# Mixing gates by seven block products inside attention, branch outputs and gates in DRAM, PSUM in single banks

## The chip, the cores and the metric

The kernel runs on one core of one Trainium2 chip. The metric is the device time of one execution in microseconds (us). The core's engines run side by side, each with an instruction queue of its own: PE (TensorE, matrix products; PEld is its weight load), DVE (VectorE), ACT (ScalarE), POOL (GpSimd) and SP (SyncE, which issues DMAs here). SBUF is the memory on the core that the engines read and write. PSUM holds what PE writes, in eight banks of 512 float32 columns on each of 128 partitions. DRAM is reached by DMA alone.

## The reference, cut to what matters

One layer works on 128 prompt tokens and 512 latent tokens of width D = 1024, all in float32:

```
h = x * (1 + scale) + shift                       # from a conditioning vector
z = h @ w_in                                      # 1024 -> 10240
hy, g_h, qkv, g_a, m = split(z)                   # 3072, 1024, 3072, 1024, 2048
y_h = hyena_long_conv(short_conv(hy))             # gated long convolution by a Fourier transform
y_a = context_attention / neighbourhood_attention # 16 heads of 64; latent queries also attend to cached keys
p_h = (y_h * silu(g_h)) @ w_bh
p_a = (y_a * silu(g_a)) @ w_ba
m_h, m_a = split(sigmoid(m))
out = (m_h * p_h + m_a * p_a) @ w_out
x_new = layer_norm(ALPHA * x + gate * out)
```

The change is about `m`: two thousand and forty-eight columns of the product `h @ w_in`, the mixing gates of the two branches.

## The kernel before, in words

**Numbers and tiles.** The 640 tokens lie in the free dimension, and features on the 128 partitions. Each float32 operand is held as two halves in a shorter format that PE takes at full rate (F32R): a high half, and the low half that is left of it. A product is three passes, high by high, high by low and low by high. The modulated input is `hH` and `hL`, each 128 x 8 x 640, where the 8 are its blocks of 128 features.

The weights are 104 tiles (`wall`) of 128 outputs by 1024 inputs. Tile numbers: 0 to 31 for the convolution inputs and `g_h`, 32 (`T_Q`) and up for queries, keys, values, `T_GA` for the attention gate, 64 to 71 (`T_MH`) and 72 to 79 (`T_MA`) for the two mixing gates, 80 to 87 (`T_BH`) for `w_bh`, 88 to 95 (`T_BA`) for `w_ba`, 96 to 103 (`T_WO`) for `w_out`. `wraw` loads a tile, 512 KB, by SP into one of two buffers; `wtile` splits it (`split`): ACT copies the high half `wh` (L98), DVE subtracts for the low half `wl` (L99). The loads wait for a free buffer, which the splitting of an older tile gives.

`proj` makes one output tile of 128 x 640 from one weight tile: for each of 8 blocks k, three passes by two halves of 320 tokens, 48 matmuls of 128 x 320 at L166, into one PSUM tile of two banks (`ps_mm`, two such tiles). It yields after each k, so that another generator's work can be put between. The other four banks (`ps_ax`) are "aux" banks, for scores, transposes and the like. `weave(main, side, n, m)` runs two generators in proportion, and so writes the program with pieces of `side` between those of `main`.

**The stages.** After a start that computes the modulation come four quarters of the convolution branch, whose results `yh0` to `yh7` stay in SBUF. Then comes attention, two heads for each j = 0 to 7 ("head j" below stands for such a pair), from 391 to 669 us. For each j, `attend(j)` is woven with plain projections, `mains(j)`: queries, keys, values and gates of coming heads, and for j = 7 the eight tiles 64 to 71 (`mix_h`), whose results stay in SBUF as `mh0` to `mh7`. In attention PE follows the written order (a `manual_schedule` for PE); the queues of DVE, ACT, POOL and SP are ordered by a scheduler from its own model, so that there an instruction can stand elsewhere than where it is written.

`attend` takes two blocks of 128 queries at a time. `tiled` writes the scores of two blocks and two heads into the four aux banks; for each, `probs` adds the bias and takes the row minimum on DVE (L803), exponentiates on ACT (L806), inverts the sum on DVE (L807) and multiplies on POOL (L808). The next step, `turned`, transposes these probabilities on PE into the same four banks, and ACT copies them out (L826). PE does 36 matmuls of `mains` between one such step and the next. `gated` (L868) multiplies a head's output by its gate into `ya0` to `ya7`, in SBUF too.

**After attention** (669 us on): two tiles of `mix_a` (72, 73) while ACT and DVE split `yh`; then eight `w_bh` tiles over `yh`, each gated by `mh`, with `ya` split beside them and the modulation's gate rows (L236) between; then eight `w_ba` tiles over `ya` with the remaining `mix_a` tiles between; then the output projection (L1065) from weights that take over the place of `hH` and `hL`, and the norm. The gate of such a tile is one ACT and one DVE instruction over both banks:

```python
ps = (yield from proj(T_MH + n))[2]                     # [2]: both banks as one tile
nc.scalar.activation(two(th), ps[:, :, :HALF], AF.Tanh, scale=0.5)
...
nc.vector.scalar_tensor_tensor(two(th), two(th), 1.0, ps[:, :, :HALF], op0=ALU.add, op1=ALU.mult)
```

Of the kernel before, what the change touches and what calls it, by code (L numbers as in the profile page):

```python
# [18 lines left out]
NK = 8  # L19
# [26 lines left out]
def tile_hyena_natten_step(ctx: ExitStack, tc: tile.TileContext, a, o):  # L46
# [44 lines left out]
    ps_mm = ctx.enter_context(tc.tile_pool(name="ps_mm", bufs=2, space=PSUM))  # L91
    ps_ax = ctx.enter_context(tc.tile_pool(name="ps_ax", bufs=4, space=PSUM))

    def aux(name):
        return ps_ax.tile([P, 512], F32, tag="aux", name=name)

# [8 lines left out]
    out = {"yh": {}}  # L105

# [48 lines left out]
    def bank(i, ps_pair=None):  # L155
        if ps_pair:
            return (*ps_pair, None)
        both = ps_mm.tile([P, 2, 512], F32, tag="mm", name=f"mm{i}")
        return both[:, 0], both[:, 1], both
# [301 lines left out]
    def conv_tile(i, dst):  # L461
        lo, hi, _ = yield from proj(i, eng="dma")
# [12 lines left out]

    def gate_tile(i, dst, eng=None):
        ps = (yield from proj(i, eng=eng))[2]
        nc.scalar.activation(two(dst), ps[:, :, :HALF], AF.Tanh, scale=0.5)
        nc.vector.scalar_tensor_tensor(two(dst), two(dst), 1.0, ps[:, :, :HALF], op0=ALU.add, op1=ALU.mult)
# [17 lines left out]
    def gate_conv(n):  # L497
        if n in half_done:
            gapped_product(out["yh"][n], out[f"u{n // 2}"][n % 2])
        half_done.add(n)  # L500
# [150 lines left out]
    yh, ident = out["yh"], out["ident"]  # L651
# [20 lines left out]
    def queries(j):  # L672
        lo, hi, _ = yield from proj(T_Q + j)
# [10 lines left out]
    def keys(j):  # L684
        raw = const.tile([P, 196], F32, tag="pack1", name=f"ck{j}")[:, :P]
        load_to(raw, a["ck"][j])
        lo, hi, _ = yield from proj(T_K + j)
# [18 lines left out]
    def values(m):  # L706
        w = [wtile(T_V + 2 * m + i, width=256) for i in range(2)]
        ps = ps_mm.tile([P, 2, 512], F32, tag="mm", name=f"v{m}")
# [7 lines left out]
        for half in range(2):  # L716
            ks = range(4 * half, 4 * half + 4)
            for k in ks:
                for x, wk, first, last in passes(k):
                    for t in range(4):  # L720
                        nc.tensor.matmul(  # L721
                            ps[:, t // 2, t % 2 * 256 : t % 2 * 256 + 256], x[:, k, P * t : P * t + P], wk,
                            start=first and t % 2 == 0, stop=last, skip_group_check=True,
                        )
                yield
            if half:
                nc.scalar.activation(v[:, :1024], ps[:].rearrange("p a b -> p (a b)"), AF.Copy)
            else:
                pe = ps_mm.tile([P, 2, 512], F32, tag="mm", name=f"ve{m}")[:, 0]
# [21 lines left out]
    ya, tms, edges, biases = [], [], {}, {}  # L751

    def attention_setup():
        nonlocal at, mask
        hy.close()
        yap = out["yap"] = tail.enter_context(tc.tile_pool(name="yap", bufs=1, side="right"))
        ya.extend(row(yap, "ya", f"ya{j}", bufs=NK) for j in range(NK))
# [15 lines left out]
    at = mask = None  # L773
# [22 lines left out]
    def probs(j, b, s, tm):  # L796
        lo, hi = TWIN[b]
        res = []
        for h in range(2):
# [3 lines left out]
            nc.vector.tensor_tensor_reduce(  # L803
                pv, s[h][:, : hi - lo], tm[h][:, lo:hi], 1.0, 3.0e38, ALU.add, ALU.min, accum_out=sm[:, 0:1]
            )
            nc.scalar.activation(pv, pv, AF.Exp, scale=-1.0, bias=sm[:, 0:1], accum_out=sm[:, 1:2])  # L806
# [60 lines left out]
    def gated(j, cols, o_):  # L867
        nc.vector.tensor_tensor(ya[j][:, cols], out[f"sg{j}"][:, cols], o_, op=ALU.mult)  # L868

    def block_values(n, o_):  # L870
# [5 lines left out]
        if b < 3:  # L876
            gated(j, slice(192 + P * b, 320 + P * b), o_)
        else:
            gated(j, slice(576, NT), o_[:, :64])
            gated(j, B7, o_[:, 64:])  # L880

    def prompt_values(j, o_):
        for h in range(2):
            pvm(o_[rows(h)], val(j, 0, h), head[j]["ptp"][:, h * P : h * P + P], True, True)
        gated(j, slice(PC, PC + LP), o_)
# [46 lines left out]
    def mix_h():  # L932
        homes = ((0, "q"), (0, "k"), (0, "v"), (), (0, "ql"), (0, "kl"), (1, "q"), (1, "ql"))
        for n in range(NK):
            th = slot(*homes[n], f"mh{n}") if homes[n] else th
            th, pair = (pair[:, NT:], None) if n == 3 else (th[:, :NT], th)
            ps = (yield from proj(T_MH + n))[2]
            nc.scalar.activation(two(th), ps[:, :, :HALF], AF.Tanh, scale=0.5)
            out[f"mh{n}"] = th
            yield  # L940

    weave(hand_over(), chain(long_conv(3), long_conv_back(3), attention_setup()), 6 * NK + N_VALUES, N_CONV + N_BACK + 1)

    def mains(j):
        if j < 3:
            return (gate_a(j + 1), queries(j + 2), keys(j + 2)), 3 * NK
        return {
            3: ((values(2), queries(5)), NK + N_VALUES),
            4: ((gate_a(4), keys(5), queries(6)), 3 * NK),
            5: ((gate_a(5), keys(6), values(3)), 2 * NK + N_VALUES),  # L950
            6: ((gate_a(6), queries(7), keys(7), gate_a(7)), 4 * NK),
            7: ((mix_h(),), 7 * NK),
# [8 lines left out]

    mp = tail.enter_context(tc.tile_pool(name="mp", bufs=1, side="right"))
    lp = left.enter_context(tc.tile_pool(name="lp", bufs=1))
    gpart = slot(1, "v", "gpart")[:, :D]
    yhH = [row(lp, "yhH", f"yhH{n}", F32R, NK) for n in range(NK)]
    yhL = []
    yaH = [row(mp, "yaH", f"yaH{n}", F32R, NK) for n in range(NK)]
    yaL = []

    def gate_rows():  # L970
        for pair in range(2):
            ps = aux(f"gate{pair}")
            for i in range(4):
                raw = wp.tile([P, D], F32, tag="raw", name=f"gate{pair}{i}")
                ada(16 + 4 * pair + i, ps[:, i * P : i * P + P], raw[:])
# [3 lines left out]
    def mix_a(n):  # L979
        ps = now(proj(T_MA + n))[2]  # L980
        th = mp.tile([P, NT], F32, tag="th", bufs=3, name=f"mta{n}")
        nc.scalar.activation(two(th[:]), ps[:, :, :HALF], AF.Tanh, scale=0.5)
# [3 lines left out]
    mtas = [mix_a(0), mix_a(1)]  # L986
    for n in range(NK):
        yhL.append(row(yhp, "yh", f"yhL{n}", F32R))
        split(yhH[n][:], yhL[n][:], yh[n][:])
    for n in range(NK):  # L990
        th = out[f"mh{n}"]
# [249 lines left out]
```

## Time and profile before

| | |
|---|---|
| median of 3 runs | 925.89 us (925.84 to 927.05) |
| the profiled execution | 925.7 us, of which the profile's span is 923.9 us |
| granted TensorE clock, mean over the span | 0.997 |
| idle time of DVE, ACT, POOL in the span | 47%, 59%, 84% |
| DMA, mean over the span | 102.13 MB, 111 GB/s |
| stages, us from the start of the span | attention 391 to 669; `mix_a` 0 and 1 to 700; `w_bh` tiles to 756; `w_ba` and the other `mix_a` to 872; output projection and norm to 924 |

The page is taken from one execution. A row of a stretch of time gives its length, and then for each engine its busy time and, in brackets, its instructions. A group row names the line, the engine, the operation and its tiles, out<-in without the numbers at their ends; "x8" is a count. In the chain each row is a start in us, a length in us, and what ran.

### The profile page before, as it was taken

The numbers are of one execution on the slowest core, as the hardware profiler recorded it, in microseconds if no ns is written. First come the engines' busy times: TensorE is split into PE (matmuls) and PEld (weight loads), VectorE is DVE, ScalarE is ACT, GpSimd is POOL, SyncE is SP. The second block draws the span as 40 slices with busy tenths as digits, with TensorE's granted clock in tenths as the row PEclk, the third lists the DMA queues.
The fourth block names the chain that finished last, engine by engine and source line by source line (L and its number), as shares of the span: only waits on it lengthen the run. The fifth ranks groups of instructions, "written<-read, shape, count | busy, mean of one in ns | idle before, by whom it ended". The sixth has DMA issues, their size and how long they took to land.

```text
span 923.9 us, 16758 instructions
## 1 busy us (share of the span) xinstructions
PE 910.2 (99%) x6856; PEld 877.4 (95%) x6856; DVE 486.4 (53%) x948; ACT 380.4 (41%) x776; POOL 146.2 (16%) x188
## 2 busy tenths in 40 slices
PE   8999999999999999999999999999999999999996
PEld 7899999999999999999999999999999999999885
DVE  4776775693796676445352533432261223335676
ACT  4485455554545334255454544444261112223200
POOL 0011010110010000474454543331000000000000
PEclk9999999999999999999999999999999999999998
DMA  8966664655465113242222221212123343224631
GB/s 320 380 161 135 128 149 98 137 133 123 100 141 126 50 49 85 86 122 67 71 68 69 67 70 58 72 49 70 48 69 113 120 146 99 72 69 116 205 114 69
DMA packets 36553, 102.13 MB, mean 111 GB/s; under 512 B 4316, under 2 KB 13020, under 8 KB 36477
## 3 DMA queue, kind: packets, MB, share of 16 engines
q1 hardware_dynamic: 32300, 86.35, 28.9%
q0 software_dynamic: 4032, 14.68, 9.8%
q8 instruction: 54, 0.88, 0.4%
q14 instruction: 23, 0.18, 0.1%
q10 hardware_dynamic: 144, 0.03, 0.0%
HBM read 97.38 MB, written 3.67 MB: 109 GB/s over the span
## 4 chain that ended last, share of the span: by engine, by line
PE 95%; DVE 2%; ACT 2%; issue 1%; POOL 0%; POOLq 0%
PE mm L166 65%; PE out L1065 6%; PE v L721 5%; PE s L788 2%; PE s L831 2%; PE pt L824 2%; PE ve L732 1%; PE adaT L236 1%; PE adaT L253 1%; PE yb L151 1%; PE yb L153 1%; PE yb L152 1%; PE gate L236 0%; PE fl L384 0%; PE fl L385 0%
## 5 line engine op out<-in xcount | busy, mean ns | idle before, releaser
L166 PE MATMUL mm<-hH,wh 128*128 128x320 f32 x1120 | 263.3, 313 | 0.9 <-ACT hH L312 0.6
L166 PE MATMUL mm<-hH,wl 128*128 128x320 f32 x1120 | 259.7, 310 | 0.4 <-DVE wl L99 0.4
L166 PE MATMUL mm<-hL,wh 128*128 128x320 f32 x1120 | 259.1, 310 | 0.0
L99 DVE TENSOR_TENSOR wl<-raw,wh 128x1024 fp32r<-128x1024 f32 x66 | 81.6, 1237 | 231.9 <-ACT wh L98 231.7
L166 PEld LDWEIGHTS mm<-hH,wh 128*128 128x128 f32 x1120 | 186.7, 188 | 6.2 <-issue 4.2
L166 PEld LDWEIGHTS mm<-hH,wl 128*128 128x128 f32 x1120 | 188.0, 188 | 1.4 <-DVE wl L99 1.1
L166 PEld LDWEIGHTS mm<-hL,wh 128*128 128x128 f32 x1120 | 188.2, 188 | 1.1 <-DVE hL L313 0.5
L98 ACT ACTIVATE wh<-raw 128x1024 fp32r<-128x1024 f32 x66 | 69.8, 1059 | 216.8 <-PE mm L166 95.9
L143 POOL DMA_DIRECT2D wl<-wall x28 | 24.3, 869 | 264.0 <-ACT wl L142 208.8
L144 ACT ACTIVATE wh<-raw 128x1024 fp32r<-128x1024 f32 x28 | 29.7, 1060 | 42.9 <-PE mm L166 42.7
L808 POOL TENSOR_SCALAR p<-p,sm 128x384 f32<-128x384 f32 x32 | 42.1, 1326 | 27.7 <-DVE sm L807 27.7
L1095 POOL TENSOR_TENSOR r<-r,bc 128x64 f32<-128x64 f32 x1 | 0.3, 320 | 249.7 <-ACT r L1094 249.7
L808 POOL TENSOR_SCALAR edge<-edge,sm 128x320 f32<-128x320 f32 x32 | 35.5, 1121 | 0.0
L474 DVE SCALAR_TENSOR_TENSOR x<-zs,pack,x 128x641 f32<-128x641 f32 x32 | 28.3, 884 | 12.1 <-ACT x L472 12.0
L826 ACT ACTIVATE pts<-pt 128x384 f32<-128x384 f32 x64 | 26.2, 502 | 11.0 <-PE pt L824 11.0
L142 ACT ACTIVATE wl<-raw 128x1024 fp32r<-128x1024 f32 x28 | 30.0, 1071 | 0.0
L166 PE MATMUL mm<-yhH,wh 128*128 128x320 f32 x128 | 29.9, 315 | 0.0
L166 PE MATMUL mm<-yaH,wh 128*128 128x320 f32 x128 | 29.2, 309 | 0.0
L166 PE MATMUL mm<-yhL,wh 128*128 128x320 f32 x128 | 29.2, 309 | 0.0
L166 PE MATMUL mm<-yaH,wl 128*128 128x320 f32 x128 | 29.2, 309 | 0.0
L166 PE MATMUL mm<-yaL,wh 128*128 128x320 f32 x128 | 29.2, 309 | 0.0
L166 PE MATMUL mm<-yhH,wl 128*128 128x320 f32 x128 | 29.2, 309 | 0.0
(330 smaller groups left out, 1677.7 us busy)
## 6 DMA issues: line engine op xcount, KB each, us to landing
raw<-wall SPq DMA_DIRECT2D x96, 512.0 KB, 3.6
wl<-wall POOLq DMA_DIRECT2D x28, 512.0 KB, 5.8
ada<-wada SPq DMA_DIRECT2D x16, 512.0 KB, 8.1
gate<-wada SPq DMA_DIRECT2D x8, 512.0 KB, 3.7
wo<-wall SPq DMA_DIRECT2D x8, 512.0 KB, 3.7
xt<-xT SPq DMA_DIRECT2D x8, 320.0 KB, 8.1
dec<-decay SPq DMA_DIRECT2D x20, 128.0 KB, 3.5
x<-xB SPq DMA_DIRECT2D x5, 512.0 KB, 3.8
```

Source lines behind the costliest of these rows:

```text
L98: hi = nc.scalar.activation(dst_h, src, AF.Copy)
L99: return hi, (eng or nc.vector).tensor_tensor(dst_l, src, f(dst_h), op=ALU.subtract)
L142: nc.scalar.activation(wl, raw[:], AF.Copy, scale=-1.0)
L143: nc.gpsimd.dma_start(wl, a["wall"][i], accum_op=ALU.add)
L144: nc.scalar.activation(wh, raw[:], AF.Copy)
L166: nc.tensor.matmul(ps[hf][:, :HALF], wt[k], x[:, hf * HALF : (hf + 1) * HALF], start=(i == 0 and k == 0), stop=(i == lead[2] and k == NK - ...
L474: nc.vector.scalar_tensor_tensor(d, zs[:, c : c + NG], convw[:, i, c : c + 1], d, op0=ALU.mult, op1=ALU.add)
L721: nc.tensor.matmul(ps[:, t // 2, t % 2 * 256 : t % 2 * 256 + 256], x[:, k, P * t : P * t + P], wk, start=first and t % 2 == 0, stop=last, ...
L788: nc.tensor.matmul(dst[h], x[rows(h), qs], y[rows(h), ks], start=i == 0, stop=i == 2, skip_group_check=True)
L808: nc.gpsimd.tensor_scalar_mul(pv, pv, sm[:, 2:3])
L826: nc.scalar.activation(ptS[:], pt[:, :384], AF.Copy)
L1065: ins = nc.tensor.matmul(dst, m[k][:, c0 : c0 + P], w[:, c : c + n], start=(first and k == 0), stop=(last and k == NK - 1), skip_group_che ...
```

## The change

Three things are altered.

*Sixteen mixing-gate tiles become eight pairs.* Two weight tiles (256 outputs) by 1024 inputs are seen as a 2 x 2 grid of blocks: a11 and a12 are the first tile's inputs 0 to 511 and 512 to 1023, a21 and a22 the second tile's. The tokens are seen so too: b11, b12 are inputs 0 to 511 of tokens 0 to 319 and of 320 to 639, b21, b22 the same tokens with inputs 512 to 1023. Strassen's scheme in Winograd's form gives the 2 x 2 result by seven block products instead of eight, from four sums of weight blocks, four sums of token blocks (`t1` to `t4`) and additions of the products. The token sums don't depend on the tile; they are made once, one half (`r` = 0 and 1) beside head 0 and head 1, and kept as high and low halves. A pair (`pair_tile`) then loads two weight tiles, makes four weight sums of 128 x 512 (L1007) and splits seven blocks (L101 on ACT, L102 on DVE), does seven products of 4 k by 3 passes into four banks x, y, v, z (the last three products are added to x, v, z), copies x out on ACT (L1041) and makes five additions on DVE (L1043, L1049) ahead of four tanh (L1061). The eight pairs stand inside attention: one beside each of heads 2 to 6, three beside head 7, where the eight tiles 64 to 71 were; nothing of tiles 72 to 79 is left after attention.

*Branch outputs and gates are kept in DRAM.* `yh` is stored after its quarter, `ya` by blocks in `gated` (L884, L885), the gates by ACT's queue (L1062); each is loaded again where it is used after attention.

*Each PSUM tile is a single bank* (`acc`, four of them in the place of two double ones), so a projection has two tiles, and what was one instruction over both banks is now two (L481 and L486 for gates).

Line numbers of the changed kernel are some 2 to 210 higher: L168 for the plain matmul, L813, L818, L819, L820 for the steps of `probs`, L1247 for the output projection. The core of the diff:

```diff
-    ps_mm = ctx.enter_context(tc.tile_pool(name="ps_mm", bufs=2, space=PSUM))
+    ps_mm = ctx.enter_context(tc.tile_pool(name="ps_mm", bufs=4, space=PSUM))
...
-    def gated(j, cols, o_):
-        nc.vector.tensor_tensor(ya[j][:, cols], out[f"sg{j}"][:, cols], o_, op=ALU.mult)
+    def gated(j, o_, *spans):
+        yo = tp.tile([P, P], F32, tag="yo", bufs=3, name=f"yo{j}")
...
+            nc.vector.tensor_tensor(yo[:, c0 : c0 + n], out[f"sg{j}"][:, cols], o_[:, c0 : c0 + n], op=ALU.mult)
+            (nc.scalar if j == 7 else nc.sync).dma_start(ya_d[j][:, cols], yo[:, c0 : c0 + n])
...
+    def token_sums(r):
...
+        tc.keep_in_program_order(nc.vector.tensor_tensor(t1, part(hH, 0, 1), part(hL, 0, 1), op=ALU.add))
+        yield
+        nc.vector.tensor_tensor(t2, t1, part(hH, 0, 0), op=ALU.subtract)
+        nc.vector.tensor_tensor(t2, t2, part(hL, 0, 0), op=ALU.subtract)
+        yield
+        keep("t1", t2)
...
+    ORDER = ("b11", "t2", "t3", "t1", "b21", "t4", "b22")
...
+        def prep(j):
+            if j > 6:
+                return
+            wb[j] = wp.tile([P, 2, 512], F32R, tag=RING[j % 5], bufs=2 if RING[j % 5] == "wh" else 3, name=f"wb{i0}_{j}")
+            split(wb[j][:, 0], wb[j][:, 1], src[j])
...
+        for j in range(7):
+            if j < 4:
+                ps["xyvz"[j]] = acc(f"sp{i0}_{j}")[:, :HALF]
+            dst, x = ps["xyvzxvz"[j]], operand(ORDER[j])
+            for k in range(4):
+                wh, wl = (wb[j][:, i, P * k : P * k + P] for i in range(2))
+                for i, (wk, xi) in enumerate(((wh, 0), (wh, 1), (wl, 0))):
+                    nc.tensor.matmul(
+                        dst, wk, x(xi, k), start=j < 4 and k == 0 and i == 0, stop=k == 3 and i == 2, skip_group_check=True,
+                    )
+                if k == 1:
+                    yield
+            if j == 0:
+                u = halfrow("u", 1, "u")
+                nc.scalar.activation(u, dst, AF.Copy)
+            elif j == 1:
+                nc.vector.tensor_tensor(u, dst, u, op=ALU.add)
+            elif j == 4:
+                use(0, 0, dst)
+            else:
+                if j != 3:
+                    c = halfrow("c", 4, f"c{j}_")
+                nc.vector.tensor_tensor(c, dst, c if j == 3 else u, op=ALU.add)
+                if j != 2:
+                    use(*{3: (1, 1), 5: (1, 0), 6: (0, 1)}[j], c)
+            prep(j + 5)
...
-            7: ((mix_h(),), 7 * NK),
+            3: ((mix(1), values(2), queries(5)), NK + N_VALUES + N_PAIR),
...
+            7: ((mix(5), mix(6), last_pair(mix(7))), 3 * N_PAIR),
...
-    mtas = [mix_a(0), mix_a(1)]
...
+        th = mixed(mh_d, n, "mh", NK)
...
-            for k in range(NK):
+            for k in (0, 1, 2, 3, 4, 6, 7, 5):
```

Three places show how instructions stand in the queues. A name is that of a tile with the numbers of the tile itself and of its allocation at its end. The first is DVE's queue beside head 0, from the second pair of score blocks on; `s2`, `s3` are scores, `p` and `edge` probabilities, `sm` row statistics. Before:

```order
L803 ISA p0_0_2_4569,sm0_0_2_4570<-s2_0_4553,tm0_4014 128x384
L803 ISA sm0_0_2_4570 128x1
L803 ISA p0_1_2_4575,sm0_1_2_4576<-s2_1_4554,tm1_4018 128x384
L803 ISA sm0_1_2_4576 128x1
L803 ISA edge30_4044,sm0_0_3_4581<-s3_0_4555,tm0_4014 128x320
L803 ISA sm0_0_3_4581 128x1
L803 ISA edge31_4046,sm0_1_3_4586<-s3_1_4556,tm1_4018 128x320
L803 ISA sm0_1_3_4586 128x1
L807 RECIPROCAL sm0_0_2_4570<-sm0_0_2_4570 128x1
L703 TENSOR_TENSOR kl2_4749<-ck2_4691,k2_4748 128x128 x2
```

In the changed kernel the same stretch of DVE's queue reads so, with `ts00` and `ts01` the token sums in the making and `t1_01`, `t3_01` low halves of finished ones:

```order
L102 TENSOR_TENSOR t1_01_4713<-ts01_4684,t1_00_4712 128x640
L813 ISA p0_0_2_4637,sm0_0_2_4638<-s2_0_4621,tm0_4073 128x384
L813 ISA sm0_0_2_4638 128x1
L813 ISA p0_1_2_4643,sm0_1_2_4644<-s2_1_4622,tm1_4077 128x384
L813 ISA sm0_1_2_4644 128x1
L956 TENSOR_TENSOR ts01_4684<-ts01_4684,hH_82 128x640
L102 TENSOR_TENSOR t3_01_4790<-ts00_4683,t3_00_4789 128x640
L712 TENSOR_TENSOR kl2_4844<-ck2_4773,k2_4843 128x128 x2
L819 RECIPROCAL sm0_0_2_4638<-sm0_0_2_4638 128x1
L956 TENSOR_TENSOR ts01_4684<-ts01_4684,hL_83 128x640
L819 RECIPROCAL sm0_1_2_4644<-sm0_1_2_4644 128x1
L813 ISA edge30_4103,sm0_0_3_4649<-s3_0_4623,tm0_4073 128x320
```

Sums of 640 columns now stand before the four reductions and between them; the key differences `kl2`, which stood behind the last of the four, stand between the second and the third.

The second place is DVE's queue beside head 7, behind the last reciprocals; `ov16` holds attention outputs. Before:

```order
L807 RECIPROCAL sm7_0_3_7475<-sm7_0_3_7475 128x1
L807 RECIPROCAL sm7_1_3_7480<-sm7_1_3_7480 128x1
L99 TENSOR_TENSOR wl68_7617<-raw68_7614,wh68_7616 128x1024
L99 TENSOR_TENSOR wl69_7690<-raw69_7687,wh69_7689 128x1024
L868 TENSOR_TENSOR ya7_4008<-sg7_7121,ov16_0_7627 128x128
L868 TENSOR_TENSOR ya7_4008<-sg7_7121,ov16_1_7628 128x128
L99 TENSOR_TENSOR wl70_7771<-raw70_7768,wh70_7770 128x1024
L99 TENSOR_TENSOR wl71_7849<-raw71_7846,wh71_7848 128x1024
```

In the changed kernel DVE's queue there holds the second and third of the last three pairs, with `u76`, `c2_76` the additions of the pair of tiles 76 and 77, and `s2_78`, `s1_78` the weight sums of the pair of 78 and 79:

```order
L1043 TENSOR_TENSOR u76_8465<-sp76_1_8470,u76_8465 128x320
L102 TENSOR_TENSOR wb76_5_8467<-raw77_8428,wb76_5_8467 128x512
L102 TENSOR_TENSOR wb76_6_8484<-s1_76_8432,wb76_6_8484 128x512
L1049 TENSOR_TENSOR c2_76_8529<-sp76_2_8487,u76_8465 128x320
L1007 TENSOR_TENSOR s2_78_8618<-raw78_8614,raw79_8616 128x512
L1007 TENSOR_TENSOR s1_78_8620<-s2_78_8618,raw79_8616 128x512
L1049 TENSOR_TENSOR c2_76_8529<-sp76_3_8531,c2_76_8529 128x320
L102 TENSOR_TENSOR wb78_0_8622<-raw78_8614,wb78_0_8622 128x512
```

The weight sums of the third pair stand between two additions of the second pair, and read `raw78` and `raw79`, which a load brings; the gating of `ya7` stands later in the queue.

The third place is PE's queue where the branch projections begin, after attention. Before, from the last matmuls of tile 73 to the first of tile 80:

```order
L166 MATMUL mm73_7990<-hL_77,wh73_7986 128x320 x2
L166 MATMUL mm73_7990<-hH_76,wl73_7987 128x320 x2
L166 MATMUL mm80_8071<-yhH0_7911,wh80_8067 128x320 x2
L166 MATMUL mm80_8071<-yhL0_8041,wh80_8067 128x320 x2
L166 MATMUL mm80_8071<-yhH0_7911,wl80_8068 128x320 x2
L166 MATMUL mm80_8071<-yhH1_7912,wh80_8067 128x320 x2
L166 MATMUL mm80_8071<-yhL1_8044,wh80_8067 128x320 x2
L166 MATMUL mm80_8071<-yhH1_7912,wl80_8068 128x320 x2
L166 MATMUL mm80_8071<-yhH2_7913,wh80_8067 128x320 x2
```

In the changed kernel PE's queue, near the end of the first two branch tiles, reads so:

```order
L168 MATMUL mm80_0_8870<-yhs14_8853,wl80_8867 128x320
L168 MATMUL mm80_1_8871<-yhs14_8853,wl80_8867 128x320
L168 MATMUL mm81_0_8945<-yhs15_8854,wh81_8941 128x320
L168 MATMUL mm81_1_8946<-yhs15_8854,wh81_8941 128x320
L168 MATMUL mm81_0_8945<-yhs14_8853,wl81_8942 128x320
L168 MATMUL mm81_1_8946<-yhs14_8853,wl81_8942 128x320
L238 MATMUL gate0_8930<-gate00_8931,st_84 32x128 x8
L168 MATMUL mm82_0_9019<-yhs0_8649,wh82_9015 128x320
L168 MATMUL mm82_1_9020<-yhs0_8649,wh82_9015 128x320
```

After attention the scheduler orders PE too. It has interleaved tiles 80 and 81, which now end together; the eight matmuls of the first gate row follow, and then tile 82; the `mix_a` tiles that stood ahead of them are gone.

More of the change, by code (lines that the diff above doesn't have):

```diff
@@ L930, in gate_a @@
         yield
[L932 to L939, printed above, removed]
[L940 to L942 removed]
+    SUMS = ("t1", "t3", "t2", "t4")
```

273 lines of the change are left out of this document (196 added, 77 removed).

## The prediction

> **What bounds the kernel now.** I read the head of the page, then the busy time of each engine, then the chain that ended last.
>
> ```profile
> span 923.9 us, 16758 instructions
> PE 910.2 (99%) x6856; PEld 877.4 (95%) x6856; DVE 486.4 (53%) x948; ACT 380.4 (41%) x776; POOL 146.2 (16%) x188
> PE 95%; DVE 2%; ACT 2%; issue 1%; POOL 0%; POOLq 0%
> PE mm L166 65%; PE out L1065 6%; PE v L721 5%; PE s L788 2%; PE s L831 2%; PE pt L824 2%; PE ve L732 1%; PE adaT L236 1%; PE adaT L253 1%; PE yb L151 1%; PE yb L153 1%; PE yb L152 1%; PE gate L236 0%; PE fl L384 0%; PE fl L385 0%
> ```
>
> TensorE is busy or on the chain nearly throughout, and two thirds of the span are the plain projections of L166. A busy PE could still be a slow PE, so I looked at what a matmul costs in the chain in order of time, and at the stages by stretches (columns: length; busy us of PE, PEld, DVE, ACT, POOL; granted clock; DMA share; GB/s).
>
> ```profile
> 405.90 10.57 PE mm L166 x72
> 485.22 1.44 PE ve L732 x12
> 487.97 5.76 PE v L721 x48
> ```
>
> ```profile
> 390.70:669.20 278.50, 277.89 (x2306) 267.74 (x2305) 105.35 (x359) 127.96 (x340) 112.07 (x121) 1.00 0.23 69
> 700.10:756.40 56.30, 56.30 (x462) 53.56 (x461) 13.31 (x14) 7.67 (x9) 0.00 (x0) 1.00 0.39 131
> 872.00:923.90 51.90, 43.60 (x212) 36.24 (x210) 35.39 (x69) 3.20 (x7) 0.93 (x2) 0.94 0.28 101
> ```
>
> A 320-column matmul costs 10.57 / 72 = 0.1468 us in a row, at clock 1.00. In attention (first row) PE idles 0.6 us of 278.5, with DVE at 38%, ACT at 46%, POOL at 40%. After attention (second row) nothing else comes near. Only the last 52 us hold 8.3 us of PE idle, and the change does not touch that code's dependencies. So the rate is PE's, and what counts is matmuls removed and waits put in their place.
>
> **What it removes.** The 16 mixing-gate tiles took 16 x 48 = 768 matmuls; eight pairs of 7 products x 4 k x 3 passes take 672, of the same 128x320 shape, each with its own weight load as before (6856 and 6856 above). 96 x 0.1468 = **14.1 us** off PE. A product sends twelve matmuls in a row into one bank, where a plain tile alternates between two. The twelve ve matmuls also share one bank, at 1.44 / 12 = 0.120 us each; the v matmuls alternate, at 5.76 / 48 = 0.120. Both ends that these rows give are nothing, so I price it at nothing; that one bank costs more all the same is a rival below.
>
> The Trainium skill, "TensorE: Matmul & The Clock Gate", section Back-to-back issue gap, gives a warm isolated gap of N/2.4 + 2.5 ns, 136 ns for 320 columns. The trace has 147, and decides. By the page the saving would be 13.0 us, and the sum below 1.1 us higher.
>
> **What it adds on DVE and ACT.** Durations: mean ns of one, by shape; the L1024 and lower rows give min/median/max.
>
> ```profile
> L1024 DVE TENSOR_TENSOR mta<-mta,mh x8: 819/821/825, 775.4 to 862.8; 128x640 f32<-128x640 f32 x8
> L99 DVE TENSOR_TENSOR wl<-raw,wh x66: 1218/1226/1651, 11.8 to 846.5; 128x1024 fp32r<-128x1024 f32 x66
> L99 DVE TENSOR_TENSOR sl<-sd,sh x20: 678/687/694, 61.2 to 318.8; 128x512 fp32r<-128x512 f32 x20
> L681 DVE SCALAR_TENSOR_TENSOR ql<-mm,q 128x320 fp32r<-128x320 f32 x6 | 2.9, 481 | 0.0
> L98 ACT ACTIVATE sh<-sd 128x512 fp32r<-128x512 f32 x20 | 12.8, 638 | 17.6 <-DVE sd L390 11.7 <-PE yb L152 5.9
> L470 ACT ACTIVATE zs<-mm 128x320 f32<-128x320 f32 x23 | 10.5, 458 | 0.0
> ```
>
> Token sums: 13 operations of 640 columns per half, 2 x 13 x 0.82 = 21.3 us of DVE. A pair: 4 weight sums and 7 low halves at 0.687, 5 result additions at 0.481: 9.96 us, against 2 x 1.23 for two plain tiles. ACT per pair: 7 x 0.638 + 5 x 0.458 = 6.8 us. Attention then runs about 277.9 - 6 x 7.05 (the mixing tiles inside the first row) + 8 x 84 x 0.1468 = 334 us of PE, with 105 + 21 + 80 - 10 + 3 = 199 us of DVE: 60%. On average that is cover enough; the places where it is not are local. Gate evacuations in two halves add 0.2 us of ACT to each of 16 tiles, under a full PE. Three edits cost nothing for the same reason: yh, ya and both gates through DRAM (about 21 MB over 500 us, 42 GB/s on 69 to 131 now; without that cover each would be one late load, the 3.7 us below), single banks (as many banks as before), and the final weights' order.
>
> **The places where PE can wait.**
>
> *Heads 0 and 1 (token sums).* After a pair of score blocks PE runs 36 matmuls, then needs all four score banks back for its transposes.
>
> ```profile
> 390.67:400.33 9.66, 9.66 (x77) 9.02 (x77) 6.31 (x26) 4.96 (x18) 6.18 (x10) 1.00 0.56 163
> 404.37 0.22 PE ptp L912 x2
> 416.47:431.50 15.03, 15.03 (x128) 14.41 (x128) 7.28 (x25) 7.47 (x24) 6.93 (x8) 1.00 0.20 61
> 431.50:436.03 4.53, 4.53 (x52) 4.17 (x53) 3.02 (x16) 2.11 (x6) 1.67 (x3) 1.00 0.24 82
> 439.81 0.22 PE ptp L912 x2
> ```
>
> Head 0: DVE ended the reductions at 400.33, 4.0 us ahead of the transposes. Nine token operations now stand before the last reduction and the ck remainder too: 9 x 0.82 + 0.5 = 7.9 us, of which 9.66 - 6.31 = 3.35 fall into DVE's idle time. 7.9 - 3.35 - 4.0 = 0.5 us of wait. Head 1: eleven token operations and two weight differences are added to 7.28 us: 7.28 + 9.0 + 1.4 = 17.7 in 15.03, 2.7 over, against 3.8 us of room (436.03 to 439.81). No wait by that count; I take 0.5 since two instructions of those fourteen can wait for loads. Each: 0 to 3.0 (3.0 if the idle time can't be used). The exponentials, queued behind the reductions on ACT, and POOL's multiplications behind them have a whole further round of slack.
>
> *Pairs beside heads 2 to 6.* A pair's last two products add into banks that DVE must have read first. By the queue's order the reductions of four score blocks (about 4.5 us) stand before that reading, which leaves some 3 us. 0.5 us in all, 0 to 2.0.
>
> *The three pairs in a row at the end.* Between 613 and 669 the attention pieces of the chain sum to 13.1 us; with 252 matmuls PE has 50 us there, DVE 29.9 for the pairs + 7.7 for the head + 4.1 for yh and the next weights = 41.7: 83%. The third pair's weight differences stand in DVE's queue ahead of a result addition of the second, and wait for a load that is issued only when the second's weights are split:
>
> ```profile
> raw<-wall SPq DMA_DIRECT2D x33, 512.0 KB, 3.7
> ```
>
> On SP those loads now stand behind six stores of yo that wait for DVE. Count for the second pair: the addition is ready about when product 7 needs its bank. I take 1.0 us, 0 (all hidden) to 4.0 (one whole load).
>
> *First branch tile.* PE starts two branch tiles interleaved, so both weight buffers come free together; the third waits for a split (1.06 + 1.23 us) under six matmuls, eight gate matmuls and four more, about 2.0 us. 0.4 us, 0 to 1.5.
>
> Sum, against the profiled execution's own 925.7 us (span 923.9): 925.7 - 14.1 + 0.5 + 0.5 + 0.5 + 1.0 + 0.4 = 914.5; the median shown is 0.2 above that execution, so **914.7**. All low ends: 911.8; all high ends: 925.3.
>
> **The rivals.**
>
> *DVE and POOL hold each other up.* Rows that speak for it:
>
> ```profile
> L808 POOL TENSOR_SCALAR edge<-edge,sm x32: 1074/1083/2013, 399.8 to 640.1; 128x320 f32<-128x320 f32 x32
> L808 POOL TENSOR_SCALAR p<-p,sm x32: 1232/1244/2252, 401.9 to 637.9; 128x384 f32<-128x384 f32 x32
> ```
>
> Most are at the median, a few run up to 1.0 us longer, and the wl row above has a maximum 0.43 us over its median. The new sums and splits all read two SBUF tiles. If each met a POOL operation with 40% (POOL's share) and waited half of it, 0.22 us: at the crowded places, 9 + 13 + 33 operations, 12 us of DVE, of which the rooms counted take some 5. 925.9 - 14.1 + 2.9 + 7 = 921.7. Against it: in attention the 30 wl average 1.25 us, hardly over the median. The Trainium skill, "SBUF — State Buffer", section Who interferes with whom, says just this: a DVE instruction with two SBUF inputs contends with a GpSimd instruction that reads SBUF, and whichever issues second is blocked until the first ends. The trace agrees that it happens, seldom so far.
>
> *Slower: PE and DVE in lockstep inside a pair.* Products 6 and 7 wait for DVE's readings of v and z, eight pairs long. If every pair lost more than (14.1 - 2.9) / 8 = 1.4 us, nothing is gained; at 2.5 us per pair the time is 925.9 - 14.1 + 2.9 + 20 = 934.7. For it: DVE obeys one queue, and what stands ahead waits for loads in two pairs. Against it: some 3 us of room in the other six.
>
> *Everything hidden.* DVE has 40% to spare on average, and all five waits vanish: 911.8.
>
> *The products don't save.* One bank costs 21 ns more per matmul (14.1 / 672): 925.9. The ve row speaks against it.
>
> **How the numbers follow.** The sum as counted, 913 to 919: 0.63. Everything hidden, 911.5 to 913: 0.11. POOL and DVE, 919 to 924: 0.13. No saving: 0.05. Lockstep: 0.08. A change under 0.2%, 1.85 us, can't be told from none here: the first three lie under 924.0, so faster 0.87, same 0.05, slower 0.08. The range 911.5 to 923.0 leaves out the last two and a little of the third, about 0.15.
>
> **What would show it.** Product matmuls 672 at 0.147 us in a row; PE busy about 896 us in a span near 913; DVE busy about 570 to 580; in the waits, PE for DVE by at most some us, at heads 0 and 1 and in the last three pairs. Wrong if those waits sum to over 10 us, if the low halves of the weights run well over 0.7 us or POOL's multiplications over 1.4 on the mean, or if the product matmuls are slower than plain ones.

## The result, and the profile after

The changed kernel takes **918.34 us** (median of 5 runs, 917.29 to 921.34) against 925.84 in the same series (5 runs, 925.36 to 927.05): a ratio of 0.9923, 95% interval 0.9903 to 0.9942. That is 7.5 us faster. The forecast was 914.7 in a range of 911.5 to 923.0. The profiled execution is the one of 918.34 us.

The head of the page of the changed kernel:

```profile
span 916.4 us, 17125 instructions
PE 896.1 (98%) x6760; PEld 863.0 (94%) x6760; DVE 566.6 (62%) x1118; ACT 408.6 (45%) x868; POOL 160.7 (18%) x188
```

PE lost 910.2 - 896.1 = 14.1 us of work, the whole of the 96 matmuls. The span lost only 7.5, so PE idles 6.6 us more. How dense the products run is seen in a stretch beside head 2, of the products' line alone (columns: length; PE busy; PEld busy; clock; DMA share; GB/s):

```profile
452.30:460.23 7.93, 7.93 (x54) 7.90 (x54) 1.00 0.45 149
```

54 matmuls in 7.93 us are 0.1469 each: a product costs what a plain matmul costs. The idle time is elsewhere. The waits of PE in the changed kernel that were not there before, from the timeline of PE (start; length; the wait before it and its releaser in brackets):

```profile
406.09 0.55 PE L836 MATMUL pt<-pack,p 128*128 128x128 f32 x3 [1.63 <-POOL p L820]
407.62 0.55 PE L836 MATMUL pt<-pack,p 128*128 128x128 f32 x3 [0.98 <-POOL p L820]
443.60 0.52 PE L836 MATMUL pt<-pack,p 128*128 128x128 f32 x3 [0.32 <-POOL p L820]
527.99 0.52 PE L836 MATMUL pt<-pack,p 128*128 128x128 f32 x3 [1.60 <-ACT ptsp L928]
743.96 0.56 PE L168 MATMUL mm<-yhs,wl 128*128 128x320 f32 x2 [0.31 <-DVE wl L102]
```

They sum to 4.84 us: 2.61 at head 0, 0.32 at head 1, 1.60 at the end of head 3, 0.31 at the first branch tiles, and none in the three pairs in a row. Four waits of the kernel before are gone, 1.26 us together:

```profile
50.67 0.57 PE L166 MATMUL mm<-hH,w 128*128 128x320 f32 x2 [0.65 <-ACT zs L470]
467.50 0.53 PE L166 MATMUL mm<-hH,wh 128*128 128x320 f32 x2 [0.18 <-DVE sm L807]
567.15 0.52 PE L824 MATMUL pt<-pack,p 128*128 128x128 f32 x3 [0.24 <-ACT ptsp L914]
605.75 0.52 PE L824 MATMUL pt<-pack,p 128*128 128x128 f32 x3 [0.19 <-ACT ptsp L914]
```

The rest, 3.1 us, lies behind PE's last matmul. The stretch from there to the end, of the kernel before and of the changed one (columns as in the prediction's rows of stretches):

```profile
915.60:923.90 8.30, 0.00 (x1) 0.00 (x0) 4.64 (x11) 0.74 (x2) 0.93 (x2) 0.65 0.18 63
```

```profile
905.00:916.40 11.40, 0.00 (x0) 0.00 (x0) 6.40 (x15) 0.73 (x2) 0.93 (x2) 0.64 0.23 82
```

DVE has four more instructions to do there. SP's timeline tells why. Before, the load of the last tile's residual `x` is issued at 895.75, behind the store of the second output tile; in the changed kernel it is issued at 902.49, behind the store of the fourth. The rows before, then those after:

```profile
889.22 0.34 SPq L1104 DMA_DIRECT2D y<-r  x1
895.75 0.33 SPq L63 DMA_DIRECT2D x<-xB  x1
900.36 12.00 SPq L1104 DMA_DIRECT2D y<-r  x2
```

```profile
890.96 0.34 SPq L1286 DMA_DIRECT2D y<-r  x1
891.40 0.38 SPq L63 DMA_DIRECT2D x<-xB  x1
902.10 0.34 SPq L1286 DMA_DIRECT2D y<-r  x1
902.49 0.42 SPq L63 DMA_DIRECT2D x<-xB  x1
```

It lands 4.3 us after its issue, when PE has ended, and DVE's residual additions of all three parts of the last tile wait for it:

```profile
906.87 1.36 DVE L1264 SCALAR_TENSOR_TENSOR r<-x,r 128x512 f32<-128x512 f32 x3 [1.41 <-DMA x<-xB]
```

So: -14.1 + 4.84 - 1.26 + 3.1 = -7.4, of the -7.5 us between the spans.

The cause of SP's order is one line of the change, `pinned[0] = True`, ahead of the loads of `yh`, which the cut diff above leaves out. With that flag `load_to` holds each load in the written order of SP's queue. It is set for the loads that follow attention and is not cleared, and so it holds the loads of `x` too: each is written behind the store of the tile before it, which waits for that tile's whole norm.

### The profile page after: what moved, and what is told of

The parts are those of the page before. It is cut to its first block, busy times and chain, and to the rows that moved or that the text cites. A ratio compares the mean times of both kernels' runs of the same rounds, so it can differ in the third digit from the quotient of the medians.

```text
span 916.4 us, 17125 instructions
## 1 busy us (share of the span) xinstructions
PE 896.1 (98%) x6760; PEld 863.0 (94%) x6760; DVE 566.6 (62%) x1118; ACT 408.6 (45%) x868; POOL 160.7 (18%) x188
## 5 line engine op out<-in xcount | busy, mean ns | idle before, releaser
L168 PE MATMUL mm<-hH,wh 128*128 128x320 f32 x864 | 204.4, 312 | 1.8 <-ACT zs L471 1.0
L168 PE MATMUL mm<-hH,wl 128*128 128x320 f32 x864 | 202.1, 310 | 0.4 <-DVE wl L102 0.4
L168 PE MATMUL mm<-hL,wh 128*128 128x320 f32 x864 | 202.3, 310 | 0.0
L168 PEld LDWEIGHTS mm<-hH,wh 128*128 128x128 f32 x864 | 144.8, 188 | 5.4 <-issue 2.5
L168 PEld LDWEIGHTS mm<-hH,wl 128*128 128x128 f32 x864 | 145.6, 188 | 1.3 <-DVE wl L102 0.9
L168 PEld LDWEIGHTS mm<-hL,wh 128*128 128x128 f32 x864 | 145.4, 188 | 1.1 <-DVE hL L315 0.5
L101 ACT ACTIVATE wh<-raw 128x1024 fp32r<-128x1024 f32 x50 | 52.8, 1058 | 93.2 <-PE mm L168 53.5
L102 DVE TENSOR_TENSOR wl<-raw,wh 128x1024 fp32r<-128x1024 f32 x50 | 61.7, 1236 | 48.5 <-ACT wh L101 47.8
L1034 PE MATMUL sp<-t,wb 128*128 128x320 f32 x384 | 60.2, 310 | 0.0
L1034 PEld LDWEIGHTS sp<-t,wb 128*128 128x128 f32 x384 | 56.9, 188 | 0.2 <-issue 0.2
L168 PE MATMUL mm<-yhs,wh 128*128 128x320 f32 x256 | 49.5, 311 | 0.0
L820 POOL TENSOR_SCALAR p<-p,sm 128x384 f32<-128x384 f32 x32 | 43.9, 1383 | 31.3 <-DVE sm L819 31.3
L1034 PE MATMUL sp<-hH,wb 128*128 128x320 f32 x192 | 48.4, 315 | 0.0
L1247 PE MATMUL out<-woh,yhs 128*128 128x512 f32 (+1 forms) x176 | 45.6, 373 | 0.0
L168 PEld LDWEIGHTS mm<-yhs,wh 128*128 128x128 f32 x256 | 40.2, 188 | 1.2 <-issue 1.2
L102 DVE TENSOR_TENSOR wb<-s,wb 128x512 fp32r<-128x512 f32 x32 | 22.5, 707 | 28.6 <-ACT wb L101 28.3
L820 POOL TENSOR_SCALAR edge<-edge,sm 128x320 f32<-128x320 f32 x32 | 40.2, 1266 | 0.0
L1247 PEld LDWEIGHTS out<-woh,yhs 128*128 128x128 f32 x176 | 32.0, 188 | 6.2
L101 ACT ACTIVATE wb<-s 128x512 fp32r<-128x512 f32 x32 | 20.2, 633 | 34.7 <-PE mm L168 21.0
```

What stands on the lines that cost most here:

```text
L101: hi = nc.scalar.activation(dst_h, src, AF.Copy)
L102: return hi, (eng or nc.vector).tensor_tensor(dst_l, src, f(dst_h), op=ALU.subtract)
L168: nc.tensor.matmul(ps[hf][:, :HALF], wt[k], x[:, hf * HALF : (hf + 1) * HALF], start=(i == 0 and k == 0), stop=(i == lead[2] and k == NK - ...
L820: nc.gpsimd.tensor_scalar_mul(pv, pv, sm[:, 2:3])
L1034: nc.tensor.matmul(dst, wk, x(xi, k), start=j < 4 and k == 0 and i == 0, stop=k == 3 and i == 2, skip_group_check=True,)
L1247: ins = nc.tensor.matmul(dst, m[k][:, c0 : c0 + P], w[:, c : c + n], start=(first and k == 0), stop=(last and k == 5), skip_group_check=True,)
```

## The experiments

Ten kernels ran. Each ratio is to the kernel before, in runs on the same chip.

**x_free.** The changed kernel, with the flag cleared ahead of the norm.

```diff
+    pinned[0] = False
     for i in range(2):
         load_to(bc[:, i], a["rows"][i + 1 : i + 2].to_broadcast([P, D]))
```

> The changed kernel, with one flag put back ahead of the final norm, so that the loads of x stand in SP's queue where they stood before (x4 behind the store of y1, not of y3). Theory 1 (the end is longer because each load of x stands behind the store of the tile before it): the time from the last matmul to the end falls from 11.4 us to about 8.3, the wait of DVE for the last x goes, 915.2 us against 918.3. Rival (the end is longer because the output projection now writes single banks in another order, or since other DMA traffic delays x): 918 us, nothing gained.

Measured: 913.86 us (913.16 to 914.56), ratio 0.9870 (0.9855 to 0.9884). The stretch behind the last matmul:

```profile
902.84:911.20 8.36, 0.00 (x1) 0.00 (x0) 4.64 (x11) 0.73 (x2) 0.93 (x2) 0.80 0.18 63
```

It is as long as before, with eleven DVE instructions again. Theory 1 holds. The medians moved by 4.5 us, more than the 3.0 of this stretch; in this execution PE's wait at head 0 is 1.47 us where the changed kernel's shows 2.61, which makes another 1.1, and the two medians come from different series.

**before_pinned.** The same line in the kernel before, set instead of cleared.

```diff
+    pinned[0] = True
     for i in range(2):
         load_to(bc[:, i], a["rows"][i + 1 : i + 2].to_broadcast([P, D]))
```

> The kernel before, with the same flag set ahead of the final norm, so that its loads of x stand behind the stores of y as in the changed kernel; nothing else is altered. Theory 1: about 3.1 us slower than the kernel before, 929 us, with DVE waiting for x at the last tile. Rival (order of those loads doesn't matter): 925.9 us.

Measured: 931.92 us (931.30 to 932.95), ratio 1.0066 (1.0051 to 1.0081): 5.9 us slower, by one flag. The direction is theory 1's, the size nearly double. The stretch behind the last matmul, the last store and load on SP, and the row of DVE's waits (total, times, longest):

```profile
916.48:931.10 14.62, 0.00 (x0) 0.00 (x0) 6.64 (x16) 0.73 (x2) 0.93 (x2) 0.59 0.32 108
```

```profile
916.83 0.34 SPq L1104 DMA_DIRECT2D y<-r  x1
917.23 0.42 SPq L63 DMA_DIRECT2D x<-xB  x1
```

```profile
DVE r L1082 <- DMA x<-xB: 14.5, 4, 4.3
```

Here the last load is issued after PE has ended altogether. With each load behind the store before it, load, norm and store form a chain of 10.5 to 12 us per tile; how far its end lies behind PE depends on where the first tile starts it. A fixed price for "the load is late" was the wrong model.

**one_input.** DVE's operations on the token sums beside head 0, with one SBUF input.

```diff
+        def tt(dst, x, y, op):
+            if r == 0:
+                return nc.vector.tensor_reduce(dst, x.unsqueeze(3), axis=mybir.AxisListType.X, op=ALU.min)
+            return nc.vector.tensor_tensor(dst, x, y, op=op)
...
-        nc.vector.tensor_tensor(t2, t1, part(hH, 0, 0), op=ALU.subtract)
+        tt(t2, t1, part(hH, 0, 0), ALU.subtract)
```

> The changed kernel, with the sixteen or so DVE operations of the token sums beside head 0 turned into reductions over one element, which read one SBUF tile instead of two and write the same 640 columns at the same places of the queue; the sums themselves are left out by that (their tiles hold copies). Theory 2 (two-input DVE operations hold up POOL's multiplications, which have no room at head 0): POOL's first four multiplications take about 1.1 and 1.25 us each again instead of 1.95 and 1.87, PE's wait of 2.6 us at 404 to 408 us falls under 0.5, 916 us. Rival (DVE is simply busy, and its reductions or reciprocals come late): the wait stays, 918.3 us.

Measured: 916.92 us (915.48 to 917.09), ratio 0.9899 (0.9885 to 0.9914). POOL's first multiplications of head 0 in the kernel before, the changed one and this one (two edge tiles, then two p tiles):

```profile
399.79 2.13 POOL L808 TENSOR_SCALAR edge<-edge,sm 128x320 f32<-128x320 f32 x2
401.91 2.77 POOL L808 TENSOR_SCALAR p<-p,sm 128x384 f32<-128x384 f32 x2
```

```profile
399.96 3.89 POOL L820 TENSOR_SCALAR edge<-edge,sm 128x320 f32<-128x320 f32 x2
403.84 3.73 POOL L820 TENSOR_SCALAR p<-p,sm 128x384 f32<-128x384 f32 x2
```

```profile
399.03 2.15 POOL L820 TENSOR_SCALAR edge<-edge,sm 128x320 f32<-128x320 f32 x2
401.15 3.34 POOL L820 TENSOR_SCALAR p<-p,sm 128x384 f32<-128x384 f32 x2
```

POOL starts at nearly the same time in all three. Against PE's first transpose of the round (404.21, 403.38 and 403.50) it starts 1.0 us later in the changed kernel than in the two others; there its two multiplications `pp` just ahead took 2.80 us instead of 1.20. In the changed kernel the four take 7.6 us instead of 4.9, and the last ends at 407.57 where PE has been waiting since 406.6. With one-input operations, which keep DVE busy just as long (row of DVE's groups in this kernel: 803 ns, against 0.82 us for two inputs), the edges are back at 1.08 us each, and PE's wait at head 0 is 0.24:

```profile
L956 DVE TENSOR_REDUCE ts<-ts 128x640 f32<-128x640 f32 x3 | 2.4, 803 | 0.0
```

Theory 2 holds, and the rival (DVE merely busy) falls. The p tiles stay long by half a microsecond; a two-input subtraction of weights is left there. Head 1 of the same run is a control, since its sums kept two inputs: its first edge tiles are as long as in the changed kernel (4.02 us for two in both).

```profile
424.77 4.02 POOL L820 TENSOR_SCALAR edge<-edge,sm 128x320 f32<-128x320 f32 x2
```

The Trainium skill, "SBUF — State Buffer", section Who interferes with whom, states that a DVE instruction with at most one SBUF input, outside the modes that use both of its ports, does not contend with GpSimd. These rows agree.

**sums_later.** Token sums of head 0 begun later.

```diff
-                return (alongside(plain, token_sums(j), 8),), 3 * NK
+                return (alongside(plain, token_sums(j), 20 if j == 0 else 8),), 3 * NK
```

> The changed kernel, with the token sums of head 0 begun later, so that all of them stand behind the last reduction of head 0 in DVE's queue. Theory 2: POOL's two edge multiplications are short again, its two p multiplications meet the first sums; PE's wait at head 0 falls from 2.6 us to 0 to 1.0; head 1's first reductions, behind the sums, have some 10 us of room, 916 to 917.3 us. Rival (the sums cost the same wherever they stand, since POOL is slowed for as long): the wait moves to head 1's transposes, 918.3 us.

Measured: 916.39 us (915.11 to 918.54), ratio 0.9892 (0.9876 to 0.9909). No wait is left at head 0. PE's waits for transposes in this kernel:

```profile
PE pt L836 <- ACT ptsp L928: 1.5, 1, 1.5
PE pt L836 <- POOL p L820: 1.1, 1, 1.1
PE pt L836 <- DVE sm L813: 1.1, 1, 1.1
```

The last two stand at head 1: 2.2 us, against 2.9 at heads 0 and 1 in the changed kernel. The rival has it mostly: the wait moved with the sums. The interval overlaps that of the changed kernel, so the time alone does not decide.

**plain_pairs.** x_free without the products.

```diff
-        return pair_tile(t0 + n0, t0 + n0 + 1, use)
...
+        for i in range(2):
+            ps = yield from proj(t0 + n0 + i)
+            for hf in range(2):
+                c = sp.tile([P, HALF], F32, tag="c", bufs=4, name=f"c{m}")[:]
+                nc.scalar.activation(c, ps[hf][:, :HALF], AF.Tanh, scale=0.5)
+                nc.scalar.dma_start(dst[n0 + i][:, CS[hf]], c)
...
-                return (alongside(plain, token_sums(j), 8),), 3 * NK
+                return (plain,), 3 * NK
```

> x_free with the seven-product pairs undone: each pair is two plain tiles of 48 matmuls at the same place beside attention, the token sums are left out, and DRAM, single banks and the tail stay as changed. If the products save what 96 matmuls cost (14.1 us) and lose only the waits seen in x_free (1.5 us at head 0, 1.5 at head 3), it takes about 11 us more than x_free: 925 us, with 6428 true matmuls and PE busy 14 us longer. Rival (part of the gain of the changed kernel comes from the new places of the mixing tiles and the split DMA): 920 us or less. Rival (DRAM traffic or single banks cost something that the products hide): over 928 us.

Measured: 925.65 us (11 runs, 925.45 to 927.03), ratio 0.9994 (0.9985 to 1.0003), as the main theory said. With x_free's 0.9870 the products are worth 0.0124 of 926, 11.5 us net. DRAM, the new places of the tiles and single banks, with the flag cleared, together make no difference that can be measured. PE's time in this kernel stands at the kernel before's:

```profile
PE 909.9 (98%) x6856; PEld 877.4 (95%) x6856; DVE 489.6 (53%) x980; ACT 384.6 (42%) x812; POOL 147.4 (16%) x188
```

**before_banks.** The kernel before with single PSUM banks alone.

```diff
-    ps_mm = ctx.enter_context(tc.tile_pool(name="ps_mm", bufs=2, space=PSUM))
+    ps_mm = ctx.enter_context(tc.tile_pool(name="ps_mm", bufs=4, space=PSUM))
...
+    def tanh(th, ps):
+        for p, cs in zip(ps, CS):
+            nc.scalar.activation(th[:, cs], p[:, :HALF], AF.Tanh, scale=0.5)
...
-        nc.scalar.activation(two(dst), ps[:, :, :HALF], AF.Tanh, scale=0.5)
...
+        tanh(dst, ps)
```

> The kernel before with single PSUM banks alone: four tiles of one bank instead of two tiles of two, and every evacuation that covered two banks made of two instructions; nothing else of the change. Expected: 926.0 us, within 1 us, since the added evacuations run under a full PE. Rival (smaller tiles come free earlier, and the 0.65 us wait at 51 us goes): 925.2 us. Rival (more instructions on ACT and DVE delay the transposes): 927.5 us or more.

Measured: 924.72 us (11 runs, 923.83 to 926.03) against 926.54, ratio 0.9981 (0.9973 to 0.9990): a small gain of 1.8 us by the ratio (0.9 to 2.5), nearest to the first rival. The wait at 51 us is gone, but the profiled execution, which took 926.01 us, shows a new one of 0.6 us for a load near it; where the gain comes from stays open.

**act_first.** x_free with ACT held to the written order around the end of each head.

```diff
-                nc.scalar.activation(ptp[:], pt[:, : 2 * P], AF.Copy)
+                tc.keep_in_program_order(nc.scalar.activation(ptp[:], pt[:, : 2 * P], AF.Copy))
...
-            split(wb[j][:, 0], wb[j][:, 1], src[j])
+            hi, _ = split(wb[j][:, 0], wb[j][:, 1], src[j])
+            if j < 3:
+                tc.keep_in_program_order(hi)
```

The wait it is about, in the changed kernel: ACT copies the high half of a weight sum, which DVE could not make before its load had landed, and only then the transposes' copy `ptsp`.

```profile
524.19 0.69 DVE L1007 TENSOR_TENSOR s<-raw,raw 128x512 f32<-128x512 f32 x1 [3.79 <-DMA raw<-wall]
525.64 0.63 ACT L101 ACTIVATE wb<-s 128x512 fp32r<-128x512 f32 x1 [1.00 <-DVE s L1007]
527.48 0.37 ACT L928 ACTIVATE ptsp<-ptp 128x256 f32<-128x256 f32 x1
```

> x_free, with ACT's queue held to the written order where a pair of heads ends: the copies of the transposed probabilities stand ahead of the high halves of the next pair's weights. Theory 3 (at 525 us PE waits since those high halves wait on ACT for a weight load, with the transposes' copies queued behind them): the wait of 1.5 us at 526 to 528 us goes, 912.3 us against 913.9. Rival (the pair's weights, now split later, make its first product late): the wait moves to the first product behind it, 913.9 us or more.

Measured: 931.02 us (929.38 to 932.30), ratio 1.0047 (1.0034 to 1.0059): 17 us slower than x_free, far beyond the rival. The wait at 526 us is gone, but the first product of six of the eight pairs now waits for its weights:

```profile
PE sp L1036 <- ACT wb L101: 9.8, 6, 2.9
PE pt L836 <- POOL p L820: 2.6, 2, 1.6
PE sp L1036 <- DVE c L1051: 1.4, 1, 1.4
PE sp L1036 <- DVE wb L102: 0.9, 5, 0.2
```

```profile
533.77 0.83 ACT L688 ACTIVATE q<-mm 128x256 fp32r<-128x256 f32 x3 [6.24 <-PE mm L168]
534.47 0.64 ACT L101 ACTIVATE wb<-raw 128x512 fp32r<-128x512 f32 x1
```

The held order put the high halves behind ACT's copies of the query tile, which PE has yet to finish: ACT idles 6.24 us ahead of them, and PE then waits 1.28 us for ACT. The new waits sum to 12.1 us (9.8 + 1.4 + 0.9) of these 17, and the old one of 1.5 is gone. A further part is PE itself, which is busy for 901.9 us against x_free's 895.6. By an estimate some 3 us of that come from one stretch behind two of the new waits (1.44 us up to 699.74, 2.89 us up to 707.67): there the granted clock is 0.50, while in the stretch with the wait of 2.12 us up to 728.37 it is 1.00 (columns as in the prediction's rows of stretches).

```profile
707.60:711.20 3.60, 3.53 (x12) 3.31 (x13) 3.55 (x6) 1.57 (x4) 3.60 (x3) 0.50 0.09 32
715.00:730.00 15.00, 12.71 (x102) 11.83 (x100) 6.08 (x12) 6.03 (x14) 0.00 (x0) 1.00 0.26 86
```

```profile
709.36 0.73 PE L1036 MATMUL sp<-hH,wb 128*128 128x320 f32 x2
709.89 0.47 PE L1036 MATMUL sp<-hL,wb 128*128 128x320 f32 x1
710.16 0.73 PE L1036 MATMUL sp<-hH,wb 128*128 128x320 f32 x2
```

Three product matmuls start in 0.80 us here, 0.267 each instead of 0.147; the 22 from 707.67 on take 6.2 us instead of 22 x 0.147 = 3.2. The rest of the 6.3 us is not assigned. Of the new waits only the 1.44 us for DVE's addition (L1051) is of the kind that the prediction calls lockstep; the others are for a first product's weights. What act_first shows is another dependence: pairs have room only as long as their weights are split ahead of the tile before them.

**both.** act_first, and the four multiplications of the first two blocks on ACT.

```diff
-            nc.gpsimd.tensor_scalar_mul(pv, pv, sm[:, 2:3])
+            if j == 0 and b < 2:
+                nc.scalar.activation(pv, pv, AF.Identity, scale=sm[:, 2:3])
+            else:
+                nc.gpsimd.tensor_scalar_mul(pv, pv, sm[:, 2:3])
```

> act_first, and besides the four multiplications of the first two blocks of head 0 made by ACT instead of POOL. Theory 2 (POOL's multiplications are what PE waits for at head 0): the wait at 404 to 408 us goes, some 1.5 us, 910.8 us. Rival (ACT, which has the exponentials and the high halves of the sums there, becomes late in its place): PE waits as long for ACT, 912.3 us.

Measured: 929.98 us (928.80 to 933.33), ratio 1.0044 (1.0027 to 1.0060). The time is act_first's, whose cost hides the rest. At head 0 the trace decides: 0.30 us of wait for DVE and 0.58 for ACT are left where act_first has 2.6 for POOL, so each theory has a part.

**pair_second.** x_free with a plain tile ahead of the pair beside head 4.

```diff
-            4: ((mix(2), gate_a(4), keys(5), queries(6)), 3 * NK + N_PAIR),
+            4: ((gate_a(4), mix(2), keys(5), queries(6)), 3 * NK + N_PAIR),
```

> x_free, with the plain tile of gate_a put ahead of the pair beside head 4, so that at the end of head 3 it is a plain tile's weights, not a pair's, that ACT and DVE prepare ahead of the transposes' copies; the pair's weights have one tile of PE's work longer to arrive. Theory 3 (the wait at 526 us is the late load of the pair's weights in ACT's queue): it goes, and none comes at the first product, 912.4 us against 913.9. Rival (any weights prepared there are as late, since the buffers come free with the value tiles): PE waits as long, for the plain tile, 913.9 us.

Measured: 912.94 us (911.25 to 917.17), ratio 0.9862 (0.9841 to 0.9883). The wait at the end of head 3 fell from 1.54 to 0.47, and none came at the first product; theory 3 holds in the trace. In time it is 0.9 below x_free, with overlapping intervals.

**pair_second_p.** The same, with the two p multiplications of block 1 at head 0 on ACT.

```diff
-            nc.gpsimd.tensor_scalar_mul(pv, pv, sm[:, 2:3])
+            if j == 0 and b == 1:
+                nc.scalar.activation(pv, pv, AF.Identity, scale=sm[:, 2:3])
...
```

> pair_second, and besides two of the four multiplications of head 0's first blocks (the p tiles of block 1) made by ACT instead of POOL. Theory 2: POOL ends its two edge multiplications by some 403 us, ahead of the transposes, and PE's wait of 1.5 to 2.6 us at head 0 falls to about 0.3, 911.2 us. Rival (ACT is late in its place, as with all four moved, where 0.9 us stayed): 911.9 us or more.

Measured: **911.45 us** (910.38 to 913.30), ratio 0.9851 (0.9837 to 0.9864), the fastest of all: 14.8 us under the kernel before. PE's waits in attention are now:

```profile
PE pt L839 <- ACT ptsp L931: 0.7, 2, 0.5
PE pt L839 <- POOL p L823: 0.2, 1, 0.2
```

0.9 us where the changed kernel had 4.5. At head 0 only 0.20 us is left, for ACT, so theory 2 holds in the trace; in time the intervals of this run and pair_second overlap. With the end behind the last matmul as before, the whole of the 14.1 us is in the time.

## Why the prediction was right, and where its steps failed

The time came out in the range and in the main case (913 to 919), 3.6 us above the sum. What carries it is the count of matmuls; that it stayed in the main case is in part luck. The terms that came out higher (head 0, the pairs, the end) add up to 6.3 us, those that came out lower, with the old waits that went, to 2.5. With the 5.9 us that the flag cost in before_pinned, in place of 3.1, the time by this estimate would have been 921, outside the main case. The signs named for being wrong stayed away: five waits of 4.84 us, low halves of 0.71 us, POOL's multiplications at 1.27 and 1.38 us in the mean (the last just under the limit of 1.4). The steps one by one:

- *96 matmuls, 14.1 us.* It came as counted: PE's busy time fell by 14.1, at 0.1469 us per product matmul (in x_free, one_input and pair_second, with the same matmuls, it is 895.6, 896.3 and 895.0). "The products don't save" falls with it, and plain_pairs bears it out from the other side.
- *Three edits cost nothing.* True of them together by plain_pairs, once the flag, which came with the loads of `yh` from DRAM, is cleared. Single banks alone were a gain of 1.8 us; so DRAM and the new places may cost about a microsecond, which no run separates.
- *"The change does not touch that code's dependencies"*, said of the last 52 us, is the step that failed most. It was read off what the tiles depend on, while a flag had moved the loads in SP's queue. Price: 3.1 us here, 5.9 in before_pinned.
- *Head 0.* 0.5 was taken, 2.61 measured, inside its 0 to 3.0, but by another path. The count of DVE's operations was sound: no transposes waited for a reduction. What failed is "POOL's multiplications behind them have a whole further round of slack". Before the change POOL ended the last of the two p tiles at 404.68 (its row stands under one_input), and PE began to transpose the two at 405.08. That is 0.4 us of slack and no round, since POOL makes bias tiles first, for whose load it idles 3.19 us up to 398.03. Two rows would have told it.

```profile
405.08 0.82 PE L824 MATMUL pt<-pack,p 128*128 128x128 f32 x6
```

- *DVE and POOL hold each other up* stood as a rival at 921.7, spread over all crowded places. It is real, but in PE's time only at heads 0 and 1, where POOL is late already; from head 2 on an edge tile takes 1.14 us in the mean, against 1.10, and PE waits for POOL nowhere.
- *Head 1.* 0.5 taken, 0.32 measured, for POOL here too.
- *Pairs beside heads 2 to 6.* 0.5 taken, 1.60 measured, inside 0 to 2.0, again by another path: not DVE late to read a bank, but ACT's copies behind a weight that waited for its load.
- *Three pairs in a row.* 1.0 taken, none measured: PE waits for no pair there, so the loads behind the stores of `yo` came in time. *First branch tile:* 0.4 taken, 0.31 measured.
- *Lockstep* did not happen: in the changed kernel PE waits for no reading of a bank by DVE. What it would have cost is not shown; act_first has one such wait, of 1.44 us.

In sum: the five waits were to cost 2.9 and cost 4.84, of which 1.26 came back from old waits, so 0.7 of the 3.6 us is theirs; the 3.1 us behind the last matmul are nearly all the rest.

## What to carry to other kernels

When an edit sets a flag or a mode, list every later instruction that passes through it: here the loads of a stage that the edit was not about went behind stores, for 3 to 6 us. Slack is to be measured on the engine that releases the wait, here POOL's end against PE's start, not on the engine that gets the new work. And a queue order that looks bad at one place may be what feeds the next: to put other work there (pair_second) was cheaper than to force the order (act_first).

## What was not expected of the hardware

POOL's multiplications of 128x320 stretched from 1.07 us to as much as 2.36 beside two-input DVE operations, while some of DVE's 640-column operations there stretched from 0.82 to 1.2 to 1.3; one-input DVE operations of the same length left the former at 1.09. Idle PE can cost more than itself: in act_first, where waits of 1.44 and 2.89 us came within 9 us, the granted clock was 0.50 behind them, and a product matmul took 0.267 us instead of 0.147. Waits of 1.0 to 2.1 us elsewhere in that run left it at 1.00. Whether it is the length or the closeness of the two waits, no run separates.

The changed kernel's time spreads over 4.1 us between runs, the kernel before's over 1.7. The late loads at the end are not the whole reason: x_free spreads over 1.4, but pair_second, with the loads as in x_free, over 5.9. PE's wait at head 0 differs between executions too (2.61, 1.47 and 1.01 us in the changed kernel, x_free and pair_second, whose instructions there are alike). What sets the spread stays open.
